# A hybrid decoder layer on one core: written order for the row factors, other places for the ada products, another last channel

## The chip, the cores and the metric

One core of one Trainium2 chip runs the whole layer; the other cores are idle. The metric is the device time of one execution in microseconds. An engine works through its own queue in order and waits on semaphores: TensorE (PE) for matmuls, VectorE (DVE), ScalarE (ACT) and GpSimd (POOL) for elementwise work, SyncE (SP) to issue DMAs.

## The reference

One decoder layer on x of 256 tokens by 1024 channels, all in float32. A conditioning row c gives nine modulation vectors of 1024: `mod = c @ w_ada + b_ada`, three each (shift, scale, gate) for three blocks.

1. FFN1: `x += 0.5 (1+g1) * swiglu(rmsnorm(x)*(1+sc1)+sh1)`, with `swiglu(h) = (silu(h Wg) * (h Wu)) Wd` and 2816 hidden columns.
2. The mixer: `x += (1+g2) * concat(o_a, o_m) @ w_out` of the normed and modulated x. Half of the width is causal attention of 8 heads of 64 (with 256 tokens and blocks of 256 no earlier block is ever chosen), followed by a row norm. The other half is an mLSTM of 4 heads of 128: a causal convolution of four taps with Silu gives x_conv; q, k, v and two gates per head follow from it; then a gated linear attention with a running maximum, a norm of each head, and `o_m = (h * mlstm_norm + mlstm_skip * x_conv) * silu(z)`.
3. FFN2 as FFN1, then a last rmsnorm.

## The kernel before

Everything lies transposed: channels on the 128 partitions, the 256 tokens along the rows, so x is 8 blocks of [128, 256]. A float32 operand of a matmul is split into a hi part that TensorE takes as fp32r and a lo part (the rest), and a product is three matmuls, hi*hi, lo*hi and hi*lo (`mm3`). The splitting of weights runs beside the matmuls: SP loads chunks of 1 MB into four `raw` buffers, ACT copies 1024 columns to `whi` (line 209) and DVE subtracts to get `wlo` (line 210), five buffers each. `weights()` (line 219) loads three chunks ahead and splits one ahead.

Each modulation column block is an *ada product* (line 247): SP loads [128, 1024] of w_ada into one of three buffers, and DVE multiplies it by the broadcast c and sums along the row. 72 of them are needed; the first 16 stand in the first half of FFN1, the other 56 wait in a list `jobs`, and `side(...)` (line 551) takes as many from it as it has arguments, at fixed places of the program. The order of the list is scale 1, gate 0, shift 1, gate 1, scale 2, shift 2, and gate 2 before FFN2; a block's gs, sh or gt is formed after its eighth product.

FFN1 starts while its inputs arrive. For the first eight hidden tiles it goes through the channel blocks from the outside (`outer`, d 0 to 3), keeps the partial sums in `half`, then does four inner chunks for the next eight tiles (d 0 to 3), outer chunks d 4 to 7 for these (line 474), and four inner chunks that complete the first eight (line 481). In this last loop `late` holds the finishing of the other eight tiles (Silu, product, hi and lo); two are taken before each chunk. PSUM has eight banks in three tags, b (2), m (2) and a (4), and `ring` gives a tag to each tile. Six more hidden tiles follow (line 506), then the down product (line 527): for each output block d, 22 pairs of a 512-column matmul (hi weight against hi and lo of the hidden tile at once) and a 256-column one (lo weight against hi). The two halves of the PSUM bank are then added to x by two DVE operations (lines 542 and 359).

`residual` also squares the new x on ACT, sums the squares on POOL, and prepares the next block's input: `pre_h` (line 330) makes hi and lo of x*gs. The norm's 1/rms is not known yet; it is multiplied in behind the matmul, and the shift is carried as two further columns (`pre_shift`), so that these products have 258 columns. In a padded row W = 258 floats lie one behind another.

In the mixer the projections fill PE between the small matmuls of attention and mLSTM. Its end is what the change touches: z tile pairs are projected (`tiles`), `m_sums` gives each head's output `cn` and row sums, `m_vars` the sums of squares, and `m_factors` (line 792) turns them into one factor per head and token, on four rows: a square on ACT, max and add on DVE, Ln and Exp on ACT, three Newton steps on DVE, and a split into hi (ACT) and lo (DVE) `rows`. `z_silu` applies Silu to two z tiles at a time, which needs another activation table than Ln and Exp. `m_out_pre` multiplies cn by its norm and silu(z), `m_spread` copies the factors to 128 partitions with four matmuls, and `m_out` (line 830) multiplies, adds the skip product and splits: that is `mix(4)` to `mix(7)` of the out product. `mix(0)` to `mix(3)` are the attention's channels, and mix 1 to 3 lie in hh and hl, the buffers that the z tiles read until their end. The out product (line 1000) goes through k = 0 to 7 in four chunks, `m_spread` stands behind k = 2, and PE keeps written order in the first two chunks (`pe.on = c < 2`).

Order: the program is traced in written order, then a planner with a timeline of its own reorders each engine's queue. `Ordered` (line 44) wraps an engine; while its `on` is set, each instruction is tied behind the one traced before it on the same engine. An instruction traced while it is off may move, also across tied ones. SP's DMAs are always tied, as is `z_silu`.

Of the kernel before, what the change touches and what calls it, by code (L numbers as in the profile page):

```python
# [17 lines left out]
P = 128  # L18
T = 256
D = 1024  # L20
ND = 8
NF = 22
W = T + 2
NH = 4
AH = 8
# [35 lines left out]
def layer(ctx: ExitStack, tc: tile.TileContext, i, out: bass.AP):  # L61
# [76 lines left out]
    warm(2)  # L138
    act.activation(c_bc[:, 0:512], pc[0], AF.Copy)
    dve.tensor_tensor(sq[:, 0:4], x_sb[:, 0:4], x_sb[:, 0:4], ALU.mult)  # L140
    dve.tensor_tensor(sq[:, 0:2], sq[:, 0:2], sq[:, 2:4], ALU.add)
    act.activation(sq[:, 4:8], x_sb[:, 4:8], AF.Square)
    act.activation(c_bc[:, 512:1024], pc[1], AF.Copy)
    dve.tensor_tensor(sq[:, 4:6], sq[:, 4:6], sq[:, 6:8], ALU.add)
# [23 lines left out]
    ohr = const([36, NH, P], F32R, "ohr")  # L168
    dve.tensor_copy(ohr, oh32)

# [68 lines left out]
    mod = const([P, 72], F32, "mod")  # L239
    b1 = const([P, 72], F32, "b1")  # L240
    dve.tensor_scalar(b1, sm[:, 0:72], 1.0, None, ALU.add)
    gs = [const([P, ND], F32, f"gs{k}") for k in range(3)]
# [69 lines left out]

    hh = const([P, ND, W], F32R, "hh")
    hl = const([P, ND, W], F32R, "hl")

# [42 lines left out]
    def residual(d, ps, g, k):  # L358
        dve.scalar_tensor_tensor(x_sb[:, d], ps, g[:, d:d + 1], x_sb[:, d], ALU.mult, ALU.add)
        if k is None:  # L360
            s = add_sq(d, pool)
            pool.tensor_scalar(fin_u[0][:, d], x_sb[:, d], sm[:, C_NF + d:C_NF + d + 1], None, ALU.mult)
            return s
        if d == ND - 1:
            s = add_sq(d, pool)
            pre_h(k, d)
        else:
            pre_h(k, d)
            s = add_sq(d, pool)
        return s  # L370
# [26 lines left out]
    def ffn(k, nxt):  # L397
        nfa = 3
        with tc.tile_pool(name=f"g{k}", bufs=1) as gp:
            g2 = gp.tile([P, NF, 2, T], F32R, name=f"g2{k}")  # L400
            gh, gl = g2[:, :, 0], g2[:, :, 1]
            if k == 0:
# [47 lines left out]
                for d in range(4):  # L450
                    ordered(d == 0)
                    if d < 3:
                        adas(d + 1)
                        load_to(d + 1)
                        fins(d + 1)
                        split_to(d + 1)
                        w = parts[d]
                        used[0] += d > 0
                    else:
                        w = weights()  # L460
                    if d == 0:
                        first(raws[0], ps, h0)
                    else:
                        outer(w, ps, d, False, keep if d == 3 else None)
                    if d == 1:
                        hilo(hh[:, 0, 0:T], hl[:, 0, 0:T], h0)
                ps = [bank(t) for t in ring]
                for j in range(4):
# [5 lines left out]
                for d in range(4, 8):  # L474
                    w = weights()
                    if d > 5:
                        side(1, 0)
                    outer(w, ps, d, d == 7)
                late = [lambda ft=ft, pb=pb: finish(gh, gl, 8 + ft, pb[:, 0:T], pb[:, T:2 * T])
                        for ft, pb in enumerate(ps)]  # L480
                for j in range(4):
                    late.pop(0)()
                    late.pop(0)()
                    w = weights()
                    side(1, 1)
                    for f2 in range(2):
                        ft = 2 * j + f2
                        pb = bank(ring[ft])
                        inner(w, f2, pb, 4, True)
                        o = half[:, ft]  # L490
                        dve.tensor_tensor(o, o, pb, ALU.add)
                        finish(gh, gl, ft, o[:, 0:T], o[:, T:2 * T])
                late = []
                nfa = 16
# [11 lines left out]
            for ft in range(nfa, NF):  # L506
# [3 lines left out]
                if late:  # L510
                    late.pop(0)()
                side(*QF[k])
                if k == 0:
                    pb = bank(ring[ft % 8])
                    for d in range(ND):
                        for g in range(2):
                            mm3(pb[:, g * T:(g + 1) * T], w, (d * 2 + g) * P, hh[:, d, 0:T], hl[:, d, 0:T],
                                start=(d == 0 and g == 0), stop=(d == ND - 1))
                    finish(gh, gl, ft, pb[:, 0:T], pb[:, T:2 * T])
                else:  # L520
                    pb = [bank("maba"[ft % 4 - 3]) for g in range(2)]
                    for g in range(2):
                        for d in range(ND):
                            mm3(pb[g][:, 0:W], w, (g * ND + d) * P, hh[:, d], hl[:, d],
                                start=(d == 0), stop=(d == ND - 1))
                    finish_pre(gh, gl, ft, pb[0], pb[1], r)
            tables("natural_log_exp_and_others")
            w, rest = None, []
            for d in range(ND):
                pd = bank(ring[d % 8])  # L530
                for ft in range(NF):
                    b = d * NF + ft
                    if b % 16 == 0:
                        w = weights()
                        side(*QD[k][b // 16 % 2])
                    hi, lo = part(w, (b % 16) * P, P)
                    pe.matmul(pd, hi, g2[:, ft], start=(ft == 0), stop=(ft == NF - 1), skip_group_check=True)
                    rest.append(lambda lo=lo, ft=ft, pd=pd: pe.matmul(
                        pd[:, 0:T], lo, gh[:, ft], start=False, stop=(ft == NF - 1), skip_group_check=True))
                    while rest and (ft < NF - 4 or ft == NF - 1):  # L540
                        rest.pop(0)()
                dve.scalar_tensor_tensor(x_sb[:, d], pd[:, T:2 * T], gt[k][:, d:d + 1], x_sb[:, d], ALU.mult, ALU.add)
                nxt_sq[0] = residual(d, pd[:, 0:T], gt[k], nxt)
# [13 lines left out]

    jobs += scale_jobs(1) + gate_jobs(0) + shift_jobs(1) + gate_jobs(1) + scale_jobs(2) + shift_jobs(2)
    ffn(0, 1)

    px = [bank("a") for _ in range(4)]
    for c in range(2):
        w = weights()
        side(1)
        for d4 in range(4):
# [9 lines left out]
    with tc.tile_pool(name="fin", bufs=1) as fp:  # L577
# [4 lines left out]
        r2 = r.unsqueeze(1).to_broadcast([P, 2, T])  # L582
        for d in range(0, ND, 2):
            dve.tensor_tensor(u[:, d:d + 2], u[:, d:d + 2], r2, ALU.mult)
            (sp, nc.scalar)[d // 2 % 2].dma_start(out[:, d:d + 2], u[:, d:d + 2])


def mixer(tc, nc, i, mp, L):
# [203 lines left out]
    def m_factors():  # L792


        prow, em = st["prow"], st["em"]
        dd = mt([NH, T], "dd", tag="R2")
        act.activation(dd, prow[0:4, 0:T], AF.Square, scale=EPS ** 0.5)
# [21 lines left out]
    def m_out_pre(h):  # L819

        dve.scalar_tensor_tensor(cn[:, h], cn[:, h], sm[:, C_MN + h:C_MN + h + 1], zs[:, h], ALU.mult, ALU.mult)
        pool.tensor_tensor(xc[:, h], xc[:, h], zs[:, h], ALU.mult)

# [144 lines left out]
    g = tiles(shifted(zs[:, 0]), shifted(zs[:, 1]))  # L968
    side(1)
    next(g)  # L970
# [13 lines left out]
    m_vars(2)  # L984
    for h in range(NH):
        act.activation(xc[:, h], xc[:, h], AF.Copy, scale=sm[:, C_SK + h:C_SK + h + 1])
    g = tiles(shifted(zs[:, 2]), shifted(zs[:, 3]))
# [4 lines left out]
    z_silu(0)  # L992
    next(g)
    z_silu(1)
    for h in range(NH):
        m_out_pre(h)
    for j in range(1, 4):
        hilo(*mix(j), oa[:, j, 0:T])
    po = [bank(t) for t in ("m", "m", "a", "a")]
    for c in range(4):  # L1000
        w = weights()
        pe.on = c < 2
        for k2 in range(2):
# [98 lines left out]
```

## Time and profile before

| what | value |
|---|---|
| time, median of 3 runs (range) | 534.91 us (534.86 to 535.97) |
| the profiled execution's own time | 537.05 us |
| its span, first to last instruction | 535.2 us |
| mean granted TensorE clock | 0.989 |
| busy: PE, DVE, ACT, POOL | 517.4, 423.4, 281.0, 46.9 us |
| busy share: PE, DVE, ACT, POOL | 97%, 79%, 53%, 9% |
| moved by DMA | 125.73 MB, mean 235 GB/s |

A row of the profile reads `engine line operation out<-in`, with the program's names; line 54 is the wrapper, so names tell operations apart. In a timeline the first number is the start in us from the span's start, the second the time from the first start to the last end of a group, and brackets hold idle time of the engine before it and what ended it. Matmuls are pipelined: a matmul lasts longer than the distance to the next. PEclk and the clock of a stretch are the granted share of 2.4 GHz.

### The profile page before, as it was taken

How to read it: one execution, taken by the hardware profiler on the slowest of the kernel's cores; microseconds unless marked ns; L12 is line 12 of the kernel's file. 1: busy time of each engine (PE TensorE's matmuls, PEld its weight loads, DVE VectorE, ACT ScalarE, POOL GpSimd, SP SyncE). 2: the span in 40 equal slices, each digit the busy share in tenths (PEclk: the TensorE clock that was granted, in tenths of full speed). 3: DMA queues.
4: the chain of work that ended last, by engine and by line, in shares of the span. 5: the costliest groups of instructions: out<-in, count | busy, mean ns of one | idle time of the engine just before them, and what ended most of it. 6: DMA issues, size and time to landing. Idle time of an engine off the chain costs nothing.

```text
span 535.2 us, 9560 instructions
## 1 busy us (share of the span) xinstructions
PE 517.4 (97%) x3804; PEld 485.3 (91%) x3804; DVE 423.4 (79%) x714; ACT 281.0 (53%) x486; POOL 46.9 (9%) x64
## 2 busy tenths in 40 slices
PE   7999999899999999999999989999999999999992
PEld 7899999899988889988987889999999999988881
DVE  7898879999889997898885686989986776655423
ACT  4464436355555544566767554865545455544410
POOL 5000000000001110110000020400000000022220
PEclk9999999899999999999999999999999999999998
DMA  8997977988778998578631024488955455455002
GB/s 311 356 411 298 381 282 294 349 351 325 300 286 329 328 344 303 172 287 319 225 146 59 15 105 141 184 326 293 312 195 186 163 196 193 157 206 188 1 1 78
DMA packets 23951, 125.73 MB, mean 235 GB/s; under 512 B 2657, under 2 KB 2913, under 8 KB 14434
## 3 DMA queue, kind: packets, MB, share of 16 engines
q1 hardware_dynamic: 23618, 124.59, 62.2%
q8 instruction: 30, 0.49, 0.4%
q10 hardware_dynamic: 288, 0.52, 0.3%
q14 instruction: 15, 0.12, 0.1%
HBM read 124.05 MB, written 1.05 MB: 234 GB/s over the span
## 4 chain that ended last, share of the span: by engine, by line
PE 89%; DVE 4%; DMA 3%; issue 2%; ACT 1%; SPq 0%; DVEq 0%; ACTq 0%
PE psa L54 42%; PE psb L54 27%; PE psm L54 21%; DMA ada<-in_ada 2%; DMA x<-in_x 1%; DVE junk L54 1%; DVE wlo L54 1%; ACT whi L54 0%; DVE cn L54 0%; DVE u_out L54 0%; ACT sq L54 0%; DVE nw L54 0%; DVE half L54 0%; ACT zs L54 0%; DVE x L54 0%
## 5 line engine op out<-in xcount | busy, mean ns | idle before, releaser
L54 ACT ACTIVATE whi<-raw 128x1024 fp32r<-128x1024 f32 (+1 forms) x160 | 167.2, 1047 | 137.8 <-PE psa L54 62.4
L54 DVE TENSOR_TENSOR wlo<-raw,whi 128x1024 fp32r<-128x1024 f32 (+1 forms) x160 | 193.3, 1211 | 53.2 <-ACT whi L54 51.8
L54 PE MATMUL psa<-hh,whi 128*128 128x258 f32 (+1 forms) x388 | 110.1, 286 | 0.6 <-DVE gm L54 0.6
L54 PE MATMUL psa<-hh,wlo 128*128 128x258 f32 (+1 forms) x388 | 110.3, 286 | 0.0
L54 PE MATMUL psa<-hl,whi 128*128 128x258 f32 (+1 forms) x388 | 108.8, 285 | 0.0
L54 PE MATMUL psb<-hh,whi 128*128 128x258 f32 (+1 forms) x316 | 91.3, 290 | 2.3 <-ACT hh L54 1.2
L54 DVE SCALAR_TENSOR_TENSOR junk<-ada,c_bc 128x1024 bf16<-128x1024 f32 x72 | 88.1, 1224 | 3.4 <-DMA ada<-in_ada 3.3
L54 PE MATMUL psb<-hh,wlo 128*128 128x258 f32 (+1 forms) x316 | 89.4, 284 | 0.0
L54 PE MATMUL psb<-hl,whi 128*128 128x258 f32 (+1 forms) x316 | 88.9, 283 | 0.0
L54 PEld LDWEIGHTS psa<-hh,whi 128*128 128x128 f32 x388 | 74.4, 192 | 0.8 <-DVE gm L54 0.8
L54 PEld LDWEIGHTS psa<-hh,wlo 128*128 128x128 f32 x388 | 74.4, 192 | 0.1
L54 PEld LDWEIGHTS psa<-hl,whi 128*128 128x128 f32 x388 | 73.9, 192 | 0.0
L54 PEld LDWEIGHTS psb<-hh,whi 128*128 128x128 f32 x316 | 59.8, 189 | 5.3 <-issue 1.4
L54 PEld LDWEIGHTS psb<-hh,wlo 128*128 128x128 f32 x316 | 59.7, 189 | 0.1
L54 PEld LDWEIGHTS psb<-hl,whi 128*128 128x128 f32 x316 | 59.7, 190 | 0.0
L54 PE MATMUL psa<-g,whi 128*128 128x512 f32 x176 | 59.4, 395 | 0.0
L54 PE MATMUL psm<-hh,wlo 128*128 128x256 f32 (+1 forms) x200 | 56.9, 285 | 0.0
L54 PE MATMUL psm<-hh,whi 128*128 128x256 f32 (+1 forms) x200 | 56.8, 284 | 0.0
L54 PE MATMUL psm<-hl,whi 128*128 128x256 f32 (+1 forms) x200 | 56.6, 285 | 0.0
L54 PE MATMUL psa<-g,wlo 128*128 128x256 f32 x176 | 45.5, 281 | 0.0
L54 PEld LDWEIGHTS psa<-g,whi 128*128 128x128 f32 x176 | 32.5, 188 | 7.2
L54 PEld LDWEIGHTS psm<-hh,whi 128*128 128x128 f32 x200 | 38.2, 191 | 0.2
(241 smaller groups left out, 768.3 us busy)
## 6 DMA issues: line engine op xcount, KB each, us to landing
ada<-in_ada SPq DMA_DIRECT2D x72, 512.0 KB, 6.0
raw<-in_dn SPq DMA_DIRECT2D x22, 1024.0 KB, 4.8
raw<-in_guB SPq DMA_DIRECT2D x19, 1024.0 KB, 4.8
raw<-in_gu SPq DMA_DIRECT2D x18, 1024.0 KB, 7.1
raw<-in_gu SPq DMA_DIRECT2D x8, 512.0 KB, 7.6
raw<-in_wqk SPq DMA_DIRECT2D x4, 1024.0 KB, 5.8
raw<-in_wout SPq DMA_DIRECT2D x4, 1024.0 KB, 4.8
raw<-in_guA SPq DMA_DIRECT2D x4, 768.0 KB, 4.5
```

The costliest lines, as they stand in the source:

```text
L54: r = f(*a, **k)
```

## The change

- FFN1: channel blocks 0 to 2 in written order on all engines (before, block 0 alone); `b1` and the second half of c's broadcast are formed earlier; `ohr` is copied by ACT.
- The ada products are taken at other places: one at each of the outer chunks d 4 to 7 (before, two at d 6 and d 7), one in the last of the four inner chunks (before, two in each), none at tile 16, two (before one) at each of the two chunks of the mixer's first product, three (before one) at the first z pair, and one at each chunk of the out product, as far as there are any. gate 0 comes ahead of scale 1.
- In the last inner loop of FFN1 the left-over tiles are finished in the order 2, 3, 6, 7, two ahead of each of the first two chunks, and 0, 1, 4, 5 at tiles 16 and 17; the inner chunks use the a banks alone, and tiles 16 to 21 a, a, a, a, b, m.
- After FFN1's down product, `pre_h` of blocks 0 to 5 stands behind the residuals of d 3, 4 and 5, two at a time.
- From `m_factors` to `m_out_pre` ACT and DVE keep written order, and the hi and lo halves of mix 1 to 3 stand before the second `z_silu`.
- `mlstm_skip * x_conv * silu(z)` is one DVE operation a head (before, a scaling on ACT and a product on POOL).
- The last output block of FFN2's down product is made with three 256-column products a tile and added to x by one operation.
- The last two output blocks are multiplied and sent one by one.
- The rows of hh and hl are 272 floats apart instead of 258.

```diff
+WS = T + 16
@@ start
-    act.activation(c_bc[:, 0:512], pc[0], AF.Copy)
+    for k in range(2):
+        act.activation(c_bc[:, k * 512:(k + 1) * 512], pc[k], AF.Copy)
...
-    act.activation(c_bc[:, 512:1024], pc[1], AF.Copy)
+    b1 = const([P, 72], F32, "b1")
+    dve.tensor_scalar(b1, sm[:, 0:72], 1.0, None, ALU.add)
...
-    dve.tensor_copy(ohr, oh32)
...
-    hh = const([P, ND, W], F32R, "hh")
-    hl = const([P, ND, W], F32R, "hl")
+    hh = const([P, ND, WS], F32R, "hh")[:, :, 0:W]
+    hl = const([P, ND, WS], F32R, "hl")[:, :, 0:W]
@@ residual
-        if d == ND - 1:
+        if k == 1:
+            s = add_sq(d, pool)
+            for j in range(2 * d - 6, 2 * d - 4) if 3 <= d < 6 else range(d, d + 1) if d >= 6 else ():
+                pre_h(k, j)
+        elif d == ND - 1:
             s = add_sq(d, pool)
             pre_h(k, d)
@@ ffn
-                    ordered(d == 0)
+                    ordered(d < 3)
...
                         hilo(hh[:, 0, 0:T], hl[:, 0, 0:T], h0)
+                        act.activation(ohr, oh32, AF.Copy)
...
                 for d in range(4, 8):
                     w = weights()
-                    if d > 5:
-                        side(1, 0)
+                    side(1)
                     outer(w, ps, d, d == 7)
-                late = [lambda ft=ft, pb=pb: finish(gh, gl, 8 + ft, pb[:, 0:T], pb[:, T:2 * T])
-                        for ft, pb in enumerate(ps)]
+                late = [lambda ft=ft: finish(gh, gl, 8 + ft, ps[ft][:, 0:T], ps[ft][:, T:2 * T])
+                        for ft in (2, 3, 6, 7, 0, 1, 4, 5)]
                 for j in range(4):
-                    late.pop(0)()
-                    late.pop(0)()
+                    if j < 2:
+                        late.pop(0)()
+                        late.pop(0)()
                     w = weights()
-                    side(1, 1)
+                    if j == 3:
+                        side(1)
                     for f2 in range(2):
                         ft = 2 * j + f2
-                        pb = bank(ring[ft])
+                        pb = bank("a")
...
-                late = []
...
-                side(*QF[k])
+                if k or ft > 16:
+                    side(*QF[k])
                 if k == 0:
-                    pb = bank(ring[ft % 8])
+                    pb = bank("aaaabm"[ft - 16])
...
+                    if nxt is None and d == ND - 1:
+                        mm3(pd[:, 0:T], w, (b % 16) * P, gh[:, ft], gl[:, ft], start=(ft == 0), stop=(ft == NF - 1))
+                        continue
...
-                dve.scalar_tensor_tensor(x_sb[:, d], pd[:, T:2 * T], gt[k][:, d:d + 1], x_sb[:, d], ALU.mult, ALU.add)
+                if nxt is not None or d < ND - 1:
+                    dve.scalar_tensor_tensor(x_sb[:, d], pd[:, T:2 * T], gt[k][:, d:d + 1], x_sb[:, d], ALU.mult,
+                                             ALU.add)
@@ layer
-    jobs += scale_jobs(1) + gate_jobs(0) + shift_jobs(1) + gate_jobs(1) + scale_jobs(2) + shift_jobs(2)
+    jobs += gate_jobs(0) + scale_jobs(1) + shift_jobs(1) + gate_jobs(1) + scale_jobs(2) + shift_jobs(2)
...
-        side(1)
+        side(1, 0)
...
-        for d in range(0, ND, 2):
-            dve.tensor_tensor(u[:, d:d + 2], u[:, d:d + 2], r2, ALU.mult)
-            (sp, nc.scalar)[d // 2 % 2].dma_start(out[:, d:d + 2], u[:, d:d + 2])
+        for n, (a, b) in enumerate(((0, 2), (2, 4), (4, 6), (6, 7), (7, 8))):
+            dve.tensor_tensor(u[:, a:b], u[:, a:b], r2[:, 0:b - a], ALU.mult)
+            (sp, nc.scalar)[n % 2].dma_start(out[:, a:b], u[:, a:b])
@@ mixer
         prow, em = st["prow"], st["em"]
+        act.on = dve.on = True
...
-        pool.tensor_tensor(xc[:, h], xc[:, h], zs[:, h], ALU.mult)
+        dve.scalar_tensor_tensor(xc[:, h], xc[:, h], sm[:, C_SK + h:C_SK + h + 1], zs[:, h], ALU.mult, ALU.mult)
...
     g = tiles(shifted(zs[:, 0]), shifted(zs[:, 1]))
-    side(1)
+    side(1, 0, 0)
...
-    for h in range(NH):
-        act.activation(xc[:, h], xc[:, h], AF.Copy, scale=sm[:, C_SK + h:C_SK + h + 1])
     g = tiles(shifted(zs[:, 2]), shifted(zs[:, 3]))
     side(1)
     next(g)
     m_vars(3)
     m_factors()
     z_silu(0)
     next(g)
+    for j in range(1, 4):
+        hilo(*mix(j), oa[:, j, 0:T])
     z_silu(1)
     for h in range(NH):
         m_out_pre(h)
-    for j in range(1, 4):
-        hilo(*mix(j), oa[:, j, 0:T])
+    act.on = dve.on = False
     po = [bank(t) for t in ("m", "m", "a", "a")]
     for c in range(4):
         w = weights()
+        side(0)
         pe.on = c < 2
```

## Rows read from the trace of the kernel before

**Rows 1.** The page, chain that ended last: shares of the span by engine.
```profile
PE 89%; DVE 4%; DMA 3%; issue 2%; ACT 1%; SPq 0%; DVEq 0%; ACTq 0%
```
**Rows 2.** What PE waited for: us in total, times, longest us.
```profile
PE psb L54 <- ACT hh L54: 1.2, 1, 1.2
...
PE psb L54 <- ACT whi L54: 1.1, 1, 1.1
```
**Rows 3.** Timeline of PE, 302 to 324: start, us, what.
```profile
309.85 0.29 PE L54 MATMUL psm<-hh,whi 128*128 128x256 f32 x1
...
315.45 0.28 PE L54 MATMUL psa<-hl,whi 128*128 128x256 f32 x1
317.30 0.70 PE L54 MATMUL psb<-rows,ohr 36*128 36x256 f32 x4 [1.57 <-DVE rows L54]
...
318.71 0.42 PE L54 MATMUL psm<-hl,whi 128*128 128x256 f32 x1
```
**Rows 4.** Stretches: span us, PE, PEld, DVE, ACT, POOL busy, clock, DMA, GB/s.
```profile
91.00:97.00 6.00, 6.00 (x52) 5.96 (x50) 6.00 (x11) 3.89 (x7) 0.00 (x0) 1.00 0.66 259
97.00:99.30 2.30, 0.57 (x4) 0.21 (x2) 2.30 (x5) 1.10 (x2) 0.00 (x0) 1.00 0.68 274
99.30:104.00 4.70, 4.70 (x26) 4.70 (x27) 4.70 (x9) 0.84 (x3) 0.00 (x0) 0.64 0.88 324
```
**Rows 5.** Timeline of ACT, 292 to 345.
```profile
304.57 0.36 ACT L54 ACTIVATE dd<-psa 4x256 f32<-4x256 f32 x1
...
305.24 1.01 ACT L54 ACTIVATE hh<-oa 128x256 fp32r<-128x256 f32 x3
...
308.97 0.40 ACT L54 ACTIVATE rs<-rs 4x256 f32<-4x256 f32 x1
309.39 1.28 ACT L54 ACT_TABLE_LOAD   x1
310.69 0.63 ACT L54 ACTIVATE zs<-zs 128x512 f32<-128x512 f32 x1
...
315.13 0.42 ACT L54 ACTIVATE rows<-rs 4x256 fp32r<-4x256 f32 x1 [1.15 <-DVE rs L54]
```
**Rows 6.** Timeline of DVE, 292 to 345.
```profile
309.54 0.41 DVE L54 SCALAR_TENSOR_TENSOR nw<-rs 4x256 f32<-4x256 f32 x1
311.35 1.95 DVE L54 SCALAR_TENSOR_TENSOR cn<-cn,sm,zs 128x256 f32<-128x256 f32 x2 [1.40 <-ACT zs L54]
...
316.26 0.89 DVE L54 TENSOR_TENSOR rows<-rs,rows 4x256 fp32r<-4x256 f32 x1
```
**Rows 7.** The chain of waits in order of time: start, us, what.
```profile
11.49 9.45 DMA ada<-in_ada
...
427.41 5.79 PE psa L54 x48
...
508.42 15.53 PE psa L54 x88
523.97 0.49 DVE x L54
```
**Rows 8.** Groups by operation and shape: count, busy us, mean ns, idle before.
```profile
L54 DVE TENSOR_TENSOR wlo<-raw,whi 128x1024 fp32r<-128x1024 f32 x156 | 190.7, 1225 | 53.2 <-ACT whi L54 51.8
...
L54 DVE SCALAR_TENSOR_TENSOR junk<-ada,c_bc 128x1024 bf16<-128x1024 f32 x72 | 88.1, 1224 | 3.4 <-DMA ada<-in_ada 3.3
...
L54 DVE TENSOR_TENSOR g<-gm,g 128x256 fp32r<-128x256 f32 x44 | 17.9, 417 | 0.0
...
L54 DVE TENSOR_TENSOR half<-half,psa 128x512 f32<-128x512 f32 x4 | 2.7, 676 | 0.0
```
**Rows 9.** Timeline of DVE, 265 to 292.
```profile
272.90 0.42 DVE L54 TENSOR_TENSOR rows<-nM,rows 4x256 fp32r<-4x256 f32 x1
...
277.55 2.69 DVE L54 SCALAR_TENSOR_TENSOR wE<-psm,nac,maskt 128x256 f32<-128x256 f32 x8 [2.57 <-PE psm L54]
```
**Rows 10.** DMA engines' busy tenths, 526 to 536 in 40 slices.
```profile
DMA  0000000000000000089999999999751000000000
```

More of the change, by code (lines that the diff above doesn't have):

```diff
@@ L239, in layer @@
     mod = const([P, 72], F32, "mod")
-    b1 = const([P, 72], F32, "b1")
-    dve.tensor_scalar(b1, sm[:, 0:72], 1.0, None, ALU.add)
     gs = [const([P, ND], F32, f"gs{k}") for k in range(3)]
```

## The prediction, made blind

> **What bounds the kernel now.** I read the chain of waits first. PE holds 89% of it [rows 1], so time can leave in two ways only: fewer or faster matmuls, or a gap on PE that closes. Then the list of what PE waited for. Three gaps in the body are over 1 us: for the hi half of the third channel block near 28 us and for a weight split near 98 [rows 2], and for the spread of the mLSTM row factors near 317, in PE's timeline [rows 3]. The stage table shows the second one from inside: in the stretch from 97.0 to 99.3 PE is busy 0.57 of 2.30 us while DVE is busy all of it, as in the 6 us before; the next 4.7 us run at a mean granted clock of 0.64, part of them at 1.2 GHz and the rest at 2.4, and hold 26 matmuls [rows 4]. Last the timelines of PE, ACT and DVE around 305 to 318 [rows 3, 5, 6], and the end of the chain [rows 7]. Everywhere else PE goes from matmul to matmul: 48 of 258 columns in 5.79 us, 88 of the down product in 15.53 us [rows 7]. What this change can win is therefore small and sits in few places: about 1.2 us near 28, 3.5 near 98, 3.3 near 317 (gap and slower clock together), and the end.
>
> The profiled execution took 537.05 us with a span of 535.2; the median of the timed runs is 534.91, 2.1 us less. I sum changes on the span and take them off the median.
>
> **FFN1, the stall near 98.** What empties PE there is a full DVE. Counted from the side calls, the old order pops 12 ada products (4 in the last two outer chunks, 8 in the four inner chunks behind them) where the new one pops 5 (one for each outer chunk, one in the last inner chunk). A product costs 1.22 us on DVE [rows 8]. An inner chunk of 48 matmuls lasts 5.7 us and asks DVE for two splits of 1.23, two half additions of 0.68 and four operations of 0.42 [rows 8]: 5.5 us by their full durations, 0.2 below the chunk. Before, two products more (2.4) and two of the left-over tiles (4 x 0.42 = 1.7) were laid on each of the four chunks; after, left-over tiles on the first two only, and one product on the last. Over the four chunks the demand falls from 38.4 to 26.6 us, against 23 us of PE. It is still above, but some 40 operations back to back overlap by perhaps 0.1 us each (an estimate), and five split buffers give PE pieces ahead, so I take it that PE no longer runs dry. The left-over tiles are finished in the order 2, 3, 6, 7, which are the four "a" banks that the inner chunks now use, so each bank should be read out before PE returns to it. Worth: the four matmuls of the stretch 97.0 to 99.3 need 4 x 0.12 = 0.5 us, 1.8 are lost; 26 at full clock need 3.1 of the 4.7 us, 1.6 are lost [rows 4]. Sum 3.4, with the edges -3.5 us. Bounds: -3.5 and 0.
>
> **Where the seven products go.** One more leaves at ft 16, so eight run later: the number done at the end of the gate and up products falls from 18 to 10, and from 34 to 26 at the end of the down product. gate 0 (jobs 1 to 8) is done before its first residual, scale 1 (16) is popped in the fourth chunk of the down product, hence the pre_h of blocks 0 to 5 now wait for residuals 3 to 5; shift 1 (24) falls in the tenth chunk, before pre_shift. None of this is read by PE before the mixer's first product, so 0. But the mixer then gets 19 products up to the z tiles instead of 14, and three more behind. SP issues their loads in written order between weight loads that are needed 20 us later, so I charge no queue. DVE has idle time behind the decay rows (2.57 us before wE) [rows 9]. I take +0.3 us, bounds 0 and +5 (a rival below).
>
> **The row factors.** Before, only the last instruction of each helper was pinned, and the planner floated others in: the four-row chain stands at the first Newton step at 309.54, then DVE does cn for two heads (1.95 us, waiting for a Silu on ACT), and the rows are out at 316.26 + 0.89 [rows 6]; PE, out of work at 315.45 + 0.12, starts the spread at 317.30 [rows 3]. Written order removes this: the three Newton steps stand together. But it puts something else in front of PE. The hi halves of mix 1 to 3 were floated to 305.24 [rows 5], 4.6 us before PE uses the first. Now they are chained on ACT behind the rows copy, the table load, Silu of the first z pair and the bias of z tile 3. PE is in written order in these chunks too, and comes to mix 1 at 309.85 [rows 3]. Step by step, with a hop of 0.05 to 0.1 between engines: a late bound takes the first Newton step as it stands (309.54); three steps of 0.41 end at 310.9, rows copy 0.42 to 311.4, table load and Silu 1.30 + 0.63 to 313.3 [rows 5], the col copy and bias of z tile 3 some 0.6 (as a rows copy and a bit, estimate), first hi half 0.4: 314.4, a gap of 4.5 us. An early bound starts at the square, 304.57 [rows 5], and lets nothing in between: five operations of 0.4 and their hops, first Newton step at 307.0, and with the same tail 311.9, a gap of 2.0. The three lo halves (1.08 us together, before inside the chain) now stand behind it, so I take the middle, 3.2 us. The gap of before was 1.85 less one matmul of 0.12, 1.7. So +1.5 us, bounds +0.3 and +2.8. The slower clock: at 318.71 a matmul takes 0.42 where it took 0.28 [rows 3]; I leave that cost as it is, since a gap as long stays. The spread itself then comes after 319 and no longer waits.
>
> On this chain stands the activation table load. In the row it starts 0.02 us behind the Exp before it (308.97 + 0.40) and the Silu follows 1.30 us later [rows 5]. The Trainium skill (ScalarE: Activation LUTs, What ACT_TABLE_LOAD costs) gives about 2.66 us for a switch, 1283 ns of load and 1380 ns of drain. By that the gap would be 1.4 us longer and the time 534.3. The trace has no such drain, and I go by the trace.
>
> The skip product: 4 scalings on ACT and 4 products on POOL become 4 operations on DVE, of 0.49 as the x row shows [rows 7]. They stand behind the hi and lo halves and ahead of the spread, where DVE waits anyway: 0, bounds 0 and +0.5.
>
> **First channel blocks in written order.** The DVE is the limit here too. The earlier b1 and the ohr copy on ACT take two small operations off DVE's way to the first norm (some 0.3 us, an estimate), but the next ada piece lands at 11.49 + 9.45 = 20.94 by the DMA queue [rows 7], so that is hidden. In written order both splits of block 1 stand ahead of the products of block 2, which wait for that landing: one split of 1.2 us [rows 8] less for block 2. But the hi half of each block now stands before its splits on ACT, and hl of block 0 comes in between, so block 3's splits start later by about as much. The 1.2 us near 28 [rows 2] shrinks and part comes back at block 3: 0, bounds -1.2 and +1.5.
>
> **Last channel and output.** Three products of 256 columns instead of one of 512 and one of 256. A pair takes 15.53 / 44 = 0.353 us; three at the row of 48 take 3 x 0.1206 = 0.362: 22 x 0.009 = +0.2 us (258 columns, so at most). One of the two x operations at the end goes, 0.49 with its hop of 0.03: -0.5 us [rows 7]. The other products and the row norm are untouched. Single tiles: the DMA engines are busy nine tenths and more from the first byte to the last [rows 10], so cutting the last piece in two leaves the same bytes in the queue; 0, bounds -0.3 and +0.3.
>
> The Trainium skill (DMA: Bandwidth & Descriptors, Anatomy of one DMA) has, for a DMA on the GpSimd path, about 2.0 us fixed and its bytes at 436 GB/s. By that a last piece of half the size, issued as late, would land 0.3 us sooner: 532.6. The busy row speaks against it, for the queue still holds earlier bytes then.
>
> **Row pitch 1088 bytes.** The matmuls that read the padded rows pass at 0.1206 us for 258 columns [rows 7], the down product, whose rows lie 1024 bytes apart, at 0.353 / 3 = 0.118 for 256: equal per column to 1%. I take 0; if that 1% were pitch, some 2,700 matmuls would give up to -3.
>
> **Sum.** FFN1 -3.5, moved products +0.3, row factors +1.5, first blocks 0, end +0.2 - 0.5, pitch 0: -2.0 us, 534.9 - 2.0 = **532.9 us**.
>
> **Rivals.** *The factor wait goes* (17%): hi halves come in time after all, or the shorter gap doesn't bring the slower clock. For it: the planner found holes for them before. Against: the written chain leaves no way past the rows copy. It removes 1.7 of gap and 1.6 of clock on top of the rest: 532.9 - 1.5 - 3.3 = 528.1. *The stall near 98 only moves* (15%): demand of 26.6 against 23 us is still too much, four "a" banks serve eight tiles, PE waits for a bank. A gap as before with the slower clock behind it: about 1.5 us won instead of 3.5, 534.9. *Pitch counts* (4%): 529.9. *The mixer's DVE runs over* (14%, the slower side): five more products before the z tiles are 6.1 us in a stage where the decay rows come at 272.90 and wE follows at 277.55 after 2.57 us of idle [rows 9]. If the rows come more than those 2.6 us later, PE, whose projection tiles are used up a few us later (an estimate), waits for the rest: 3.5 us and 1.6 of slower clock, 538.0. *The forecast* has 50%, its own range 531 to 534.5.
>
> 0.2% is 1.07 us, about what a measurement of this kernel can tell from no change. Faster by more: most of the forecast, the first and third rival, 66%; slower: the last rival and the late bound of the factors with a stall kept at 98, 16%; within, 18%. Range 528.0 to 536.5.
>
> **What would show it.** Right: no PE wait for a split near 98 and the clock at full there; a PE wait on ACT's hi half at mix 1 near 308 in the new times, none on the rows; one x operation after the last down matmul; same output queue. Wrong: a gap at the spread as before, a PE wait in 275 to 300, a clock drop in FFN1, cadence below 0.118 on the padded rows.

## The result, and the profile after

The changed kernel took 542.21 us (median of 4 runs, 540.89 to 543.66), the kernel before 535.44 beside it: a ratio of 1.0120, interval 1.0096 to 1.0144, 6.4 us slower, where 532.9 was forecast. The profiled execution after took 542.25 us with a span of 540.5.

The chain of waits looks as before [rows 1]; nothing in it says slower:

```profile
PE 89%; DVE 4%; DMA 2%; ACT 2%; issue 1%; SPq 0%; DVEq 0%; ACTq 0%
```

What PE waited for (us in total, times, longest) tells more. These waits begin at the modelled end of the matmul before; the gaps named in the text are counted as in the prediction, from 0.12 us behind its start, so 4.2 and 4.8 of the list are gaps of 4.4 and 4.9. The wait near 98 and the one for rows are gone [rows 2, 3]; two longer ones stand in their place:

```profile
PE psm L55 <- DVE wE L55: 4.9, 2, 4.2
PE psm L55 <- ACT hh L55: 4.8, 1, 4.8
```

The stage table of after (span, then PE, PEld, DVE, ACT and POOL busy, clock, DMA, GB/s) shows the three places:

```profile
97.00:99.30 2.30, 2.30 (x22) 2.30 (x21) 2.30 (x5) 0.81 (x1) 0.00 (x0) 1.00 0.88 367
...
277.60:282.00 4.40, 0.25 (x3) 0.05 (x1) 4.40 (x12) 2.57 (x11) 0.00 (x0) 0.97 0.32 105
282.00:285.20 3.20, 2.95 (x8) 2.30 (x8) 3.20 (x12) 2.91 (x10) 0.00 (x0) 0.51 0.93 370
311.60:316.50 4.90, 0.19 (x2) 0.00 (x0) 2.96 (x6) 4.15 (x8) 0.00 (x0) 0.94 0.27 84
316.50:322.70 6.20, 6.15 (x28) 6.15 (x29) 4.26 (x11) 1.73 (x4) 0.00 (x0) 0.50 0.16 63
```

Where PE did 4 matmuls from 97.0 to 99.3 [rows 4] it now does 22. But it stands dry from 277.6 to 282 with DVE busy throughout, and from 311.6 to 316.5, and runs at half clock behind both.

By PE's timeline the mixer's first product starts at 202.19 instead of 208.36, 6.2 us ahead. The lead is lost on the mLSTM's decay chain: DVE and ACT make four rows of the running maximum (`rows<-nM`), PE spreads them over the partitions (`psm<-rows`), DVE forms `wE` from these PSUM banks, and PE waits for that. DVE's timeline:

```profile
266.80 1.21 DVE L55 SCALAR_TENSOR_TENSOR junk<-ada,c_bc 128x1024 bf16<-128x1024 f32 x1
...
270.13 1.20 DVE L55 SCALAR_TENSOR_TENSOR junk<-ada,c_bc 128x1024 bf16<-128x1024 f32 x1
...
274.13 1.20 DVE L55 SCALAR_TENSOR_TENSOR junk<-ada,c_bc 128x1024 bf16<-128x1024 f32 x1
...
276.23 0.41 DVE L55 TENSOR_TENSOR rows<-nM,rows 4x256 fp32r<-4x256 f32 x1
...
278.15 1.22 DVE L55 SCALAR_TENSOR_TENSOR junk<-ada,c_bc 128x1024 bf16<-128x1024 f32 x1
...
279.29 1.23 DVE L55 TENSOR_TENSOR wlo<-raw,whi 128x1024 fp32r<-128x1024 f32 x1
...
280.62 2.67 DVE L55 SCALAR_TENSOR_TENSOR wE<-psm,nac,maskt 128x256 f32<-128x256 f32 x8
```

Ada products (`junk`) and a weight split stand between the steps of the decay chain. The decay rows come 74.0 us after the mixer's start instead of 64.5 [rows 9], wE 78.4 instead of 69.2. The ada products from the mixer's start to the rows (count, shortest, median and longest ns, first and last start) and the same stretch in the columns of the stage table, before and after:

```profile
L54 DVE SCALAR_TENSOR_TENSOR junk<-ada,c_bc x14: 1206/1216/1225, 211.1 to 262.6; 128x1024 bf16<-128x1024 f32 x14
208.36:272.90 64.54, 64.54 (x504) 58.75 (x504) 57.20 (x119) 40.76 (x90) 4.75 (x7) 1.00 0.67 250
```
```profile
L55 DVE SCALAR_TENSOR_TENSOR junk<-ada,c_bc x19: 1202/1218/1230, 204.9 to 274.1; 128x1024 bf16<-128x1024 f32 x19
202.19:276.23 74.04, 74.04 (x565) 66.00 (x564) 65.86 (x134) 44.95 (x98) 7.33 (x8) 1.00 0.71 265
```

Five products more (6.1 us) and one weight split more (17 instead of 16, 1.2 us) are most of the 8.7 us by which DVE is busy longer ahead of the rows. Its idle time there, 7.3 us before and 8.2 after, took up none of it. Three products of the 22 are written behind the first pair of z tiles. The last three start at 278.15, 283.38 and 286.35, so the planner put one of them, and a split, ahead of wE itself. PE had spread the rows by then and stood dry:

```profile
277.12 0.73 PE L55 MATMUL psm<-rows,ohr 36*128 36x256 f32 x4
282.05 2.95 PE L55 MATMUL psm<-qk,xc 128*128 128x256 f32 x8 [4.20 <-DVE wE L55]
```

The second gap is on ACT. Its timeline, answering to [rows 5]:

```profile
309.05 1.04 ACT L55 ACTIVATE whi<-raw 128x1024 fp32r<-128x1024 f32 x1
310.00 0.40 ACT L55 ACTIVATE rs<-vv 4x256 f32<-4x256 f32 x1
...
311.83 1.06 ACT L55 ACTIVATE whi<-raw 128x1024 fp32r<-128x1024 f32 x1 [0.98 <-PE psa L55]
312.79 0.40 ACT L55 ACTIVATE rows<-rs 4x256 fp32r<-4x256 f32 x1
313.21 1.28 ACT L55 ACT_TABLE_LOAD   x1
314.50 0.63 ACT L55 ACTIVATE zs<-zs 128x512 f32<-128x512 f32 x1
315.04 0.15 ACT L55 ACTIVATE col<-psb 128x1 f32<-128x1 f32 x1
315.68 0.51 ACT L55 ACTIVATE zs<-ht,col 128x256 f32<-128x256 f32 x1 [0.49 <-DVE ht L55]
316.10 1.01 ACT L55 ACTIVATE hh<-oa 128x256 fp32r<-128x256 f32 x3
```

and PE's, answering to [rows 3]:

```profile
311.51 0.28 PE L55 MATMUL psa<-mix0l,whi 128*128 128x256 f32 x1
316.55 0.58 PE L55 MATMUL psm<-hh,whi 128*128 128x256 f32 x1 [4.75 <-ACT hh L55]
```

The hi half of mix 1, at 305.24 before, 4.6 us before PE came to it [rows 5], now starts at 316.10, 4.6 us after mix 0 has been issued. The spread, at 325.18, no longer waits.

In the chain, the 48 matmuls of 256 columns of an FFN1 tile, the 48 of 258 of an FFN2 tile, the last two channels and the single x operation (start, us), answering to [rows 7]:

```profile
129.33 5.61 PE psb L55 x48
...
427.34 5.75 PE psm L55 x48
...
513.99 15.46 PE psa L55 x110
...
529.48 0.49 DVE x L55
```

and the output transfers of after (KB each, median us from issue to landing):

```profile
out<-u_out ACTq DMA_DIRECT2D x1, 128.0 KB, 3.5
out<-u_out SPq DMA_DIRECT2D x1, 128.0 KB, 3.4
```

### The profile page after: what moved, and what is told of

It is laid out like the page before. It is cut to its first block, busy times and chain, and to the rows that moved or that the text cites. A ratio compares the mean times of both kernels' runs of the same rounds, so it can differ in the third digit from the quotient of the medians.

```text
span 540.5 us, 9607 instructions
## 1 busy us (share of the span) xinstructions
PE 516.9 (96%) x3826; PEld 484.0 (90%) x3826; DVE 424.1 (78%) x717; ACT 282.6 (52%) x484; POOL 46.2 (9%) x60
## 4 chain that ended last, share of the span: by engine, by line
PE 89%; DVE 4%; DMA 2%; ACT 2%; issue 1%; SPq 0%; DVEq 0%; ACTq 0%
PE psa L55 45%; PE psb L55 25%; PE psm L55 20%; DMA ada<-in_ada 2%; DVE junk L55 1%; ACT whi L55 1%; DVE wE L55 1%; DVE wlo L55 0%; DVE ht L55 0%; DVE u_out L55 0%; SPq L98 0%; ACT hh L55 0%; ACT L55 0%; ACT zs L55 0%; DVE nw L55 0%
## 5 line engine op out<-in xcount | busy, mean ns | idle before, releaser
L55 PE MATMUL psa<-hh,wlo 128*128 128x256 f32 (+1 forms) x452 | 127.2, 282 | 0.0
L55 PE MATMUL psa<-hh,whi 128*128 128x256 f32 (+1 forms) x452 | 127.0, 283 | 0.0
L55 PE MATMUL psa<-hl,whi 128*128 128x256 f32 (+1 forms) x452 | 126.1, 281 | 0.0
L55 PEld LDWEIGHTS psa<-hh,wlo 128*128 128x128 f32 x452 | 85.9, 190 | 0.1
L55 PEld LDWEIGHTS psa<-hh,whi 128*128 128x128 f32 x452 | 85.7, 190 | 0.0
L55 PEld LDWEIGHTS psa<-hl,whi 128*128 128x128 f32 x452 | 85.5, 190 | 0.0
L55 PE MATMUL psb<-hh,whi 128*128 128x258 f32 (+1 forms) x284 | 81.6, 288 | 0.6 <-ACT whi L55 0.6
L55 PE MATMUL psb<-hh,wlo 128*128 128x258 f32 (+1 forms) x284 | 80.2, 283 | 0.6 <-DVE wlo L55 0.6
L55 PE MATMUL psb<-hl,whi 128*128 128x258 f32 (+1 forms) x284 | 79.8, 283 | 0.0
L55 PE MATMUL psa<-g,whi 128*128 128x512 f32 (+1 forms) x198 | 59.8, 369 | 0.0
```

The costliest lines, as they stand in the source:

```text
L55: r = f(*a, **k)
```

## The experiments

Ratios are to the kernel before, run beside each; 0.1% is 0.54 us.

**Fewer products in the mixer.** In the changed kernel, FFN1's down product takes 28 instead of 16:

```
-    QD = (((1,), (1, 0)), ...
+    QD = (((1, 1, 1), (1, 1)), ...
```

> The changed kernel, with 28 instead of 16 ada products in FFN1's down product, so that 10 instead of 22 are left to the mixer. Theory (the mixer's VectorE runs over): the 22 products, 1.2 us each, stand in front of the decay rows and wE, and PE runs dry between 277 and 286. With 12 fewer (14.6 us of VectorE) wE comes before PE wants it: the gaps of 4.4 and 1.1 us and the stretch at half clock behind them (1.7 us) go, 542.2 - 7.2 = 535.0 (534 to 537). Rival (the decays are late because projections and gates set their pace, not the products): PE waits for wE as before, 541.5 to 543. Second rival (12 more products upset the down product, where PE now has no gap): a new PE wait for a split in 128 to 200, over 538.

535.72 us, ratio 1.0012 (0.9996 to 1.0029): 5.8 us of the loss gone. PE no longer waits for wE. DVE:

```profile
265.07 0.41 DVE L55 TENSOR_TENSOR rows<-nM,rows 4x256 fp32r<-4x256 f32 x1
...
270.76 2.69 DVE L55 SCALAR_TENSOR_TENSOR wE<-psm,nac,maskt 128x256 f32<-128x256 f32 x8
```

The rows come 62.7 us after the mixer's start, with 14 products ahead of them as in the kernel before. A new wait of 1.0 us near 222 (PE for DVE's `ht`) is the price.

**The factors' order undone** (no `on` in `m_factors`; mix 1 to 3 behind `m_out_pre`), in the changed kernel:

> The changed kernel, with the row factors as before: not in written order, mix 1 to 3 split behind the products with the Silu. Theory (the written order puts the hi halves of mix 1 to 3 behind the rows copy, the table load, Silu and the last tile's bias): the hi halves float ahead again, PE's wait of 4.9 us at mix 1 becomes one of 1.7 to 1.9 at the spread, and the stretch at half clock goes from 6.8 to 3.4 us: 542.2 - 3.1 - 1.7 = 537.4 (536.5 to 539). Rival (the late stage is late for what came before it, decays and sums, whatever the order): the gap stays over 4 us, 541.5 to 543.

540.00 us, 1.0072 (1.0052 to 1.0093): 2.6 us, less than the 4.8 expected. The wait of 4.8 became one of 0.9 at the spread, and 1.5 came up at mix 4. The clock gave nothing back in the trace: half clock lasts 10.24 us behind wE and not 3.41, as much as the changed kernel has in its two stretches. Four of the eleven executions took 537.4 to 537.6, as expected. At mix 4 ACT held a split that waited for a free buffer in front of the hi halves that PE waited for; without that split, in the better order below, 0.7 of the 1.5 stays:

```profile
323.97 1.06 ACT L55 ACTIVATE whi<-raw 128x1024 fp32r<-128x1024 f32 x1 [3.46 <-PE psa L55]
324.94 1.01 ACT L55 ACTIVATE hh<-ht 128x256 fp32r<-128x256 f32 x3
```

**Mix 1 to 3 ahead of the factors.** Here they overwrite blocks of hh that the last z tile still reads, so that tile is computed from other numbers:

> The changed kernel, with the splits of mix 1 to 3 written ahead of the row factors (both still in written order). Theory: PE has mix 1 to 3 at hand when it comes there, so the wait of 4.9 us goes; the row factors come 1 to 1.5 us later for the three hi halves on ACT, but PE has 96 matmuls (11.5 us) of mix 0 to 2 before the spread, so nothing waits there either or up to 1 us: 542.2 - 4.9 - 3.4 = 533.9 (533.5 to 536). Rival (the factors now come too late and the wait moves to the spread, as in the kernel before): a PE wait of 1.5 to 4 us at the spread with 3.4 us at half clock, 536 to 540.

541.98 us, 1.0099 (1.0066 to 1.0131), a miss. The wait at mix 1 went, but the last z tile waited 0.8 and 0.4 us and mix 4 again 1.5; four of six executions took 542 with a mean clock of 0.98, two 538.3 with 0.992. It says only that the place of the hi halves made the long wait.

**The pitch, both ways:** `WS = T + 2` in the changed kernel, and only `WS = T + 16` in the kernel before.

> The changed kernel, with the norm rows 1032 bytes apart as before. Theory (pitch counts): 256-column matmuls that read hh or hl in FFN1 pass at 119.5 ns instead of 117.2, some 1,056 of them, so the mixer's first product starts 2.4 us later (204.6 instead of 202.2); FFN2's gate and up products go from 119.8 to 120.5 ns. The mixer waits for VectorE anyhow and gives part of it back: 542.2 + 0.7 to + 3.3. Rival (the 6.2 us of lead come from the closed stall, the first blocks and bank order alone): cadence and start of the mixer as in the changed kernel, 541.5 to 543.

> The kernel before with one edit, the norm rows 1088 instead of 1032 bytes apart. Theory (pitch counts): with the pitch undone in the changed kernel the mixer's first product came 2.5 us later, so here it comes 2.5 us earlier than 208.36; VectorE had 2.57 us idle behind the decay rows, so the mixer keeps it, and FFN2 adds 0.5 to 1: 534.8 - 2.5 - 0.7 = 531.6 (530.8 to 532.5). Rival (the lead is lost in the mixer, as it was in the changed kernel): 533.8 to 535.

547.48 us, 1.0218 (1.0191 to 1.0245), and 531.66, 0.9928 (0.9908 to 0.9948). Both say that the pitch counts, 3.9 us in the kernel before. In the changed kernel it is 5.3, more than the 3.3 that the expectation allows; half clock behind wE lasts 10.24 us in that trace, 3.41 with the new pitch. The same 48 matmuls of FFN1 in the chain of the changed kernel with the old pitch, of the kernel before, and of the kernel before with the new pitch:

```profile
131.72 5.73 PE psb L55 x48
```
```profile
135.35 5.73 PE psb L54 x48
```
```profile
132.06 5.61 PE psb L55 x48
```

0.12 us per 48 over 22 tiles is 2.6 us, by which the mixer's start moved in the changed kernel (204.73 and 202.19). In the kernel before it moved 3.5, to 204.86; but there the trace with the new pitch has no stretch at half clock, where the one with the old has 3.41 us near 100 and again near 318. So a part of the 3.9 may be the clock's.

**Both suspects undone together** (28 products, factors not in order):

> The changed kernel with both suspects undone: 28 ada products in the down product, and the row factors not in written order. Theory (these two are the whole loss): no wait for wE, the wait of 4.9 us at mix 1 gone, and the two smaller ones that the kernel with the factors alone undone showed left, 1.0 us at the spread and 1.6 us at mix 4: 535.7 - 4.9 + 2.6 = 533.4, less what the clock gives back (6.8 us at half: 3.4): 530.0 to 533.4, taken 531.5. Rival (a third loss of some 5 us that neither of them holds): 534.5 or more.

531.88 us, 0.9932 (0.9914 to 0.9951), near the 531.5 taken: nothing as large is left to find.

**The products' part alone, on the kernel before,** with 22 left to the mixer, and the same with 28 products in the down product:

> The kernel before with the spreading of ada products and gating alone (FFN1's side calls, order and banks of the tiles, the mixer's side calls), nothing else. Theory (closing the stall in FFN1 is worth 3.6 us and the products that it pushes into the mixer cost more): the mixer starts 3.6 us earlier, at 204.8, and wE comes 79.9 us after that, as in the changed kernel, at 284.7 instead of 281.8, with PE dry for 4 us or more and 3.4 us at half clock: 534.8 + 2.9 + 1.2 = 538.9 (537 to 540). Rival (the moved products cost nothing here): 531 to 532.

> The kernel before with FFN1's part of the change alone (side calls, order and banks of its tiles) and 28 ada products in the down product, so that the mixer has 10. Theory (FFN1's part is a gain once the mixer is not charged for it): the mixer starts 4.5 us earlier, at 203.9, and keeps it, the wait of 1.75 us for the row factors stays: 534.8 - 4.5 = 530.3 (529.8 to 532). Rival (the mixer gives the lead back, or the down product pays for 12 products more): 533 or more.

542.48 us, 1.0128 (1.0102 to 1.0153), above the 537 to 540 expected: this edit alone makes as much as the whole loss, with the wait of after, and half clock behind it for 10.24 us where 3.4 were taken:

```profile
PE psm L54 <- DVE wE L54: 4.9, 2, 4.2
```

and 534.65, 0.9980 (0.9969 to 0.9991), on the rival's side. So the 12 products moved back (by the traces 14 instead of 19 ahead of the rows) are worth 1.5%, 7.9 us, half clock included. But FFN1's lead of 4.8 us at the mixer's start shrinks to 2.3 by mix 0: 0.9 in a wait near 222, the rest in no wait of 0.1 us or more. That stays open.

**How many fit, and where.** 16 products in the mixer; then 22 with the last eight tied behind wE (`dve.on` around those side calls, three with either pair of z tiles):

> The changed kernel with 22 ada products in the down product, so that 16 are left to the mixer (14 before, 22 changed, 10 in the kernel that lost its wait). Theory (VectorE has some 2.5 us of slack ahead of wE, and only what goes beyond it is paid): two more than before fit, PE waits for wE 0.5 us at most, time as with 10 products: 535.7 (535 to 537). Rival (every product ahead of the decays is paid): 6 products of 1.2 us less 2.5 us of slack, a wait of 3 us or more and a slower clock behind it, 538.5 to 541.

> The changed kernel with the same 22 ada products in the mixer, the last 8 of them held in written order behind the work on wE (2 with the second values, 3 with either pair of z tiles). Theory (it is the place of the products, ahead of the decay chain, and not their number): wE no longer late by more than 0.5 us, 542.2 - 5.5 - 1.7 = 535.0; three products near the row factors may cost up to 2.5 there: 535 to 537.5. Rival (VectorE is full over the whole mixer): the waits come back between 285 and 320 and the time stays over 539.

537.78 us, 1.0042 (1.0027 to 1.0058): between the two ranges. PE waits 0.5 us for wE, but also 1.3 for `xc` near 244, and the rows come 70.1 us after the mixer's start; the slack is smaller than I took it for. And 538.99, 1.0070 (1.0055 to 1.0086), above the 535 to 537.5 expected; but with 22 products PE has no wait for wE at all, so their place makes that wait. Three of them got in front of the factors, where the wait at mix 1 grew to 6.6:

```profile
299.63 1.22 DVE L55 SCALAR_TENSOR_TENSOR junk<-ada,c_bc 128x1024 bf16<-128x1024 f32 x1
...
301.43 1.22 DVE L55 SCALAR_TENSOR_TENSOR junk<-ada,c_bc 128x1024 bf16<-128x1024 f32 x1
...
304.05 1.21 DVE L55 SCALAR_TENSOR_TENSOR junk<-ada,c_bc 128x1024 bf16<-128x1024 f32 x1
...
306.81 0.41 DVE L55 SCALAR_TENSOR_TENSOR nw<-rs 4x256 f32<-4x256 f32 x1
```

**The written order of the factors alone, on the kernel before:**

> The kernel before with the written order of the row factors alone (mix 1 to 3 split behind the first Silu, all of it in written order; the skip product, the ada products, the row pitch as before). Theory (the written order costs by itself what taking it out gave back): PE waits 4.9 us at mix 1 instead of 1.7 at the spread, and runs at half clock for 6.8 us instead of 3.4: 534.8 + 3.2 + 1.7 = 539.7 (538 to 540.5). Rival (it costs that much only behind the late mixer, and else what was forecast, 1.5): 535.5 to 537.

539.69 us, 1.0073 (1.0049 to 1.0098), with the same wait:

```profile
PE psm L54 <- ACT hh L54: 4.8, 1, 4.8
```

That the time agrees to the tenth is luck. The expectation counted 4.9 us from 534.8; beside the kernel before it is 3.9. And half clock behind the wait lasts 3.41 us in this trace, not 6.8. What the run shows is the longer gap, 4.9 instead of 1.7.

**A better order of the late stage,** with 28 products:

```
     m_vars(3)
-    m_factors()
-    z_silu(0)
+    w0 = weights()
+    rs, vv = m_factors()     # to Exp; Newton and rows below
     next(g)
-    for j in range(1, 4):
+    newton(rs, vv, [NH, T], "r", 0.0)
+    hilo(*mix(1), oa[:, 1, 0:T])
+    spread(rs)
+    for j in (2, 3):
         hilo(*mix(j), oa[:, j, 0:T])
+    z_silu(0)
     z_silu(1)
...
+        act.on = c in (1, 2)
+        w = weights() if c else w0
+        act.on = False
```

and `act.on` around `m_out`.

> The changed kernel with 28 ada products in the down product and another written order of the late stage: Ln and Exp of the factors, the last z tile, Newton, mix 1, rows, mix 2 and 3, table load, both Silus; weight splits that wait for a free buffer stand on ScalarE behind the Silus and behind mix 4 to 7. Theory: what PE waited for was only the place in ScalarE's order, so neither mix 1 nor the spread nor mix 4 is late by more than 0.5 us and the clock stays up: 535.7 - 4.9 - 3.4 = 527.4 (526.5 to 529). Rival (the stage is full and the wait only moves to the spread or to mix 4): a PE wait of 1.5 us or more after 303, 529.5 to 533.

530.10 us, 0.9894 (0.9875 to 0.9913). ACT now has the hi half of mix 1 at 305.08, 2.1 us after mix 0 began, and rows and table load behind it:

```profile
305.08 0.40 ACT L55 ACTIVATE hh<-oa 128x256 fp32r<-128x256 f32 x1
305.88 0.42 ACT L55 ACTIVATE rows<-rs 4x256 fp32r<-4x256 f32 x1 [0.40 <-DVE rs L55]
306.21 0.71 ACT L55 ACTIVATE hh<-oa 128x256 fp32r<-128x256 f32 x2
306.93 1.28 ACT L55 ACT_TABLE_LOAD   x1
```

No wait at mix 1 or at the spread, 0.7 left at mix 4, full clock from 6.5 to 522. It is 2.7 us slower than taken: 0.7 is mix 4, and 1.0 was never there to win, since in the kernel that it was made from the half-clock stretch (308.9 to 315.7) began 2.0 us before PE resumed, and so cost 2.4 and not 3.4. The last 1.0 I can't name.

**The first blocks as before,** in that kernel, `ordered(d == 0)`; then once more with the ohr copy tied in place:

> The best kernel so far (28 products in the down product, new order of the late stage), with only channel block 0 of the first four in written order, as before. Theory (the written order of blocks 1 and 2 costs, as the mixer's start says: 204.73 with it and 203.87 without, at the same row pitch): gaps of 0.6, 0.5 and 0.4 us near 27 to 34 become one of 0.7, the mixer starts 0.8 us earlier: 530.1 - 0.8 = 529.3 (528.9 to 529.8). Rival (it only moves, or the mixer gives it back): 529.8 to 530.5.

> The best kernel so far with only channel block 0 in written order, as in the run that missed, but with the copy of ohr on ScalarE held behind the split of block 0, where the written order has it: in the run that missed it had moved up ahead of the copies of c, and waited there 3.3 us for POOL. Theory (that copy was the miss, and the written order of blocks 1 and 2 costs 0.9 us at the mixer's start): the start as in the best kernel, one gap of 0.5 to 0.7 us near 27 instead of three, 530.1 - 0.9 = 529.2 (528.8 to 529.7). Rival (the order of blocks 1 and 2 makes no difference at the end): 529.8 to 530.5.

531.06 us, 0.9924 (0.9907 to 0.9940), a miss made by the experiment: the free copy moved up and held ACT for POOL, in front of the copies of c:

```profile
6.89 0.63 ACT L55 ACTIVATE ohr<-oh 36x512 fp32r<-36x512 f32 x1 [3.34 <-POOL oh L55]
7.43 1.05 ACT L55 ACTIVATE c_bc<-psm 128x512 f32<-128x512 f32 x2
```

With the copy tied: 529.43 us, 0.9878 (0.9852 to 0.9903), the fastest kernel here, 0.7 us below the one it was made from; the intervals overlap, the mixer's start (201.76 against 202.22) agrees in sign.

## Why the prediction was wrong

**Moved products: the step that failed.** Forecast +0.3, measured +5.8 in the changed kernel and +7.9 on the kernel before. The step counted the products right (19 instead of 14 stand ahead of the rows) and drew on the wrong slack: "DVE has idle time behind the decay rows". The row itself says what ended that idle time: PE, with the product that spreads these rows [rows 9]. It was a wait inside the chain and not room beside it. The window that mattered was the one ahead of the rows; there DVE was busy 8.7 us longer, 7.3 of it for the five products and the split, and none of its idle time was used, so the rows fell back 9.5 us against the mixer's start and PE stood dry for 4.4 and 1.0 us. The step also priced "three more behind" at nothing, though the side calls are not tied and the planner may move them; one got in front of wE. The rival "the mixer's DVE runs over" had the place and the mechanism (wE late, PE dry, clock down), with 14%, and 538.0 was still short of it. Of the prediction's own signs of being wrong two came: a PE wait in 275 to 300, and 116.9 ns on the padded rows.

**Row factors: mis-sized.** Forecast +1.5, measured +0.73%, 3.9 us, alone. The late bound (a gap of 4.5) was the right one; the gap was 4.9. Counted from the first Newton step (311.27 after) it left out the hop through DVE between the col copy and the bias, 0.5 us on ACT. Taking the middle of the bounds had no row behind it. "I leave that cost as it is" for the clock is not settled: half clock lasts 6.8 us in the trace of after, but 3.4, as before, with the factors' order alone.

**FFN1: right.** The stall is gone, and the mixer starts 4.5 to 4.8 us earlier by it than in the trace of before, which has a half-speed stretch behind the stall. The trace with the factors' order alone has the same FFN1 and stall, but no such stretch, and starts the mixer at 206.67: from there the lead is 2.8 to 3.1. The forecast was 3.5; only 0.2% of the time is left of it at the end.

**Pitch: mis-sized.** Forecast 0 with a rival of -3 at 4%; measured -0.72%, 3.9 us. I compared 258 columns of one stage with 256 of another, 120.6 and 118 ns; the 256-column matmuls on the padded rows themselves, 5.73 / 48 = 119.4 ns, were in the chain and were not read. After, they take 116.9.

**First blocks: 0 forecast, about +0.7 measured**, not clear of noise. **Skip product: forecast 0**, not measured by itself; in the trace of after its DVE operations stand behind the wait at mix 1, and the spread after them doesn't wait.

**End.** One x operation went: PE's wait for the last square fell from 1.2 to 0.7 us. The last two channels take 15.46 us instead of 15.53, so the +0.2 was 0. Single tiles: from the last row product's end to the end of the span 4.2 us instead of 4.0; the pieces of half the size took 3.4 and 3.5 us to land, no less than the whole ones (2.8 to 3.0 before). That is within the bounds, but the busy row does not stay at nine tenths to the last byte, as the prediction reads it: its last three slices are 7, 5 and 1 [rows 10]. The rule weighed there (the Trainium skill, DMA: Bandwidth & Descriptors, Anatomy of one DMA) is stated for GpSimd's path, and these transfers are issued by SP and ACT; by it, as an estimate, the last one would have landed 0.3 us sooner. The trace doesn't bear that out. The table switch again cost no drain: the load starts 0.02 us behind the instruction before it and the Silu 1.29 us later, where the Trainium skill (ScalarE: Activation LUTs, What ACT_TABLE_LOAD costs) would have about 2.66.

The parts alone, on the kernel before, add up: products and FFN1 +1.28%, factors +0.73%, pitch -0.72%, together +1.29% against +1.20% measured, with the first blocks and the end near 0 between them. But they are not independent: undone one at a time in the changed kernel, products and factors give back 1.08% and 0.48%, both together 1.88%.

## What to carry to other kernels

Work laid into "idle" time of an engine is free only if it stands behind the chain that another engine waits for. Read what ended the idle time: if it was that chain, there is no room in it. Measure the slack ahead of the chain, and where a planner may move the work, count it at the worst place. Before a helper is put in written order, list what will stand between its last input and the instruction that PE waits for, table loads and splits waiting for buffers too. When a layout changes, compare the same shape in the same stage.

## What the runs showed of the hardware that was not expected

- Rows of a moving operand 1088 instead of 1032 bytes apart: 256-column matmuls at 116.9 instead of 119.4 ns, 258-column ones at 119.8 instead of 120.6. The traces show where the 256-column ones lose it: with 1032 bytes those of odd channel blocks follow each other at 121.1 ns and those of even blocks at 118.2 (kernel before, 8 groups of 48 in FFN1, in written order); with 1088 it is 116.5 and 117.3 (changed kernel, 12 groups). Why is not shown.
- The stretch at half clock (1.2 GHz) behind a PE gap is not fixed by the gap in these traces. Behind the 4.9 us at mix 1 it lasted 6.83 us in four traces and 3.41 in one; behind the 4.4 for wE 3.41 in two and 10.24 in three; behind 1.7 to 1.8 at the spread 3.41 in two and nothing in two.
